# Layer B of a two-layer chunk-causal encoder: short value-product matmuls issued one by one between 512-column projection matmuls

## The chip, the cores and the metric

The kernel runs on one core of one Trainium2 chip, in one launch. The metric is the device time of that launch in microseconds; the number given is the median of several runs. One further execution was taken with the hardware profiler, and all rows of the profile come from that one.

## The reference, cut to what matters

Two layers are applied to 2048 prompt frames and 64 sample frames of width 1024. Each layer projects the normalised input to queries, keys, values and a gate, attends within a band of chunks of 64 frames, multiplies with the gate and projects back with a residual. Layer A has 16 query heads on 2 key heads and looks back 2 chunks; layer B, which the change names, has 16 heads of its own and looks back 8 chunks. For one chunk:

```python
s = jnp.einsum('bqkgd,bskd->bkgqs', qg, k).astype(jnp.float32) * (dh ** -0.5)
s = s + bias.reshape(kv, g, tq, tk)
p = jax.nn.softmax(s, axis=-1)
o = jnp.einsum('bkgqs,bskd->bqkgd', p.astype(v.dtype), v)   # the value product
y = x + (o * silu(gate)) @ w_out
```

Everything is float32. The kernel splits each factor into a high and a low part and adds up products of the parts, two or three matmuls for each product.

## The kernel before, in words

Tokens are handled in units of 256 (two tiles of 128), eight for the prompt, and a ninth unit of one tile with the 64 sample frames, which comes just ahead of the last prompt unit. Layer B runs eight passes, one for each pair of heads; in a pass it goes through the nine units. Each (pass, unit) is an item of the list `its`.

Two streams share TensorE, and the kernel writes TensorE's order out by hand (`tc.manual_schedule`); the orders on the other engines come from the scheduler. The first stream is the **filler** (`Filler`, L603): a list of jobs, each a generator that issues projection matmuls. `project` (L458) makes one tile's projection: eight blocks of the width, in each a high-by-high, a high-by-low and a low-by-high matmul of 512 columns (L473, L474, L475), 24 for a tile; for the sample tile the two parts of the input stand side by side in one operand and there are two matmuls for a block (L466 or L469, and L467). After each block the generator yields its cost, 3 x 512 / 2400 = 0.64 planner units, so `filler.step()` issues three matmuls at a time. `filler.done` counts the cost so far, `it.mark` is the count at which an item's projection is complete, and `filler.to(mark)` steps until the count is reached. When `filler.attending` is false, each step also drains some of the queued background work (`bg.drain`, L639).

The second stream is the attention of layer B (`pipeline`, L1189). An item has four heads in this sense (two tiles by two heads; the sample item two). For each of them the pipeline issues `scores` (L1070: matmuls L1100 and L1101, then a reduction on VectorE L1104 and an exponential on ScalarE L1108), then filler up to a first goal, then `values` for the head before (L1125: transposes L585 into the PSUM tile `sb`, split into high and low parts by ScalarE L557 and VectorE L558), then, after every second head, `outputs` (L1153), then filler up to a second goal. After head 1 of an item `queries` of the next one follows (L1032). A goal (L1209) is the smaller of two lines: from the count at the item's start, `c0`, to `end`, and, in the first four half-steps of an item, from `c0` to the mark of the item after next (`near`). `PACE_B` = 2.45 planner units for each head sets `end`, so an item of four heads asks for 9.8; `end` is at least the mark of the item after next.

`outputs` makes the value product of one head for a unit: for each tile of keys two matmuls, with the high part (L1178) and the low part (L1179) of the weights. Key tiles that both query tiles see take 256 columns. Up to two key tiles are seen by one query tile only: they take 128 columns and come last, two or four matmuls in a call. For the sample unit all six have 64 columns, and the last two of them have 64 rows, since the last block of keys is 64 long. For the second head of a pair `outputs` first transposes the gate (`tp`), and it ends with `finish_pairs` (L966): ScalarE copies (L971), VectorE additions (L973), a multiplication on GpSimd and a store.

In layer A the same filler runs under the attention of that layer (`pipeline`, L929), which places `values`, `keys`, `turned` and `outputs` at 0.3, 0.6, 0.8 and 0.95 of the way between two marks. After the attention of layer B the filler runs alone to its end with the output projection (L1301 to L1303, 264 columns).

Of the kernel before, what the change touches and what calls it, by code (L numbers as in the profile page):

```python
# [15 lines left out]
P = 128  # L16
D = 1024
KC = 8
# [30 lines left out]
NS = 4  # L49

@with_exitstack
def hybrid_encoder_kernel(
# [32 lines left out]
    nc = tc.nc  # L85
# [372 lines left out]
    def project(tile_, xc, w, C, res, ps=None):  # L458
        tt, t0, n = tile_
        ps = ps or psum("pj", 512, 2)  # L460
        for k in range(KC):
            wh, wl = weights_of(w, k)
            xh, xl = xc.parts[k // 2]
            if xl is None:
                if k == 0:
                    nc.tensor.matmul(ps[:, :C], xh[:, k % 2, :], wh, start=True, stop=False)  # L466
                nc.tensor.matmul(ps[:n, :C], xh[:, k % 2, :n], wl, start=False, stop=False)  # L467
                if k > 0:
                    nc.tensor.matmul(ps[:, :C], xh[:, k % 2, :], wh, start=False, stop=k == KC - 1)  # L469
                cost = 2 * C / 2400  # L470
            else:
                xh, xl = (a[:, k % 2, t0 : t0 + n] for a in (xh, xl))
                nc.tensor.matmul(ps[:n, :C], xh, wh, start=k == 0, stop=False)  # L473
                nc.tensor.matmul(ps[:n, :C], xh, wl, start=False, stop=False)  # L474
                nc.tensor.matmul(ps[:n, :C], xl, wh, start=False, stop=k == KC - 1)  # L475
                cost = 3 * C / 2400
            if k < KC - 1:
                yield cost
        res.append(ps)
        return cost  # L480

    def scaled(layer, tt, n, dst, ps):
        sc = rr[layer][:, tt : tt + 1]
# [162 lines left out]
    filler = Filler()  # L646
    finished = {}

    def layer_a():
# [4 lines left out]
        def add_unit(qd, place, unit):  # L654
            u, T, tiles = unit
            mine = []
            for tl in tiles:
                it = Item()
# [54 lines left out]
            def first():  # L713
                xc = st.x.pop((qd, u))
                pk = [psum("o", 512, 1), psum_a("sa", 512, 4)]
                kvs, qgs = [[], []], [[], []]
                yield from both([project(it.tile, xc, st.wkv, 256, o, ps) for it, o, ps in zip(mine, kvs, pk)])
                bias_vectors_a()
                keep(0)
                yield 2 * 3 * 256 / 2400  # L720
                for i, c in enumerate(both([project(it.tile, xc, st.w[qd], 512, o) for it, o in zip(mine, qgs)])):
                    if i == 7:
                        token_scales(unit, xc, psum("tp", 512, 1))
                        for it, o in zip(mine, kvs):
                            take_kv(it, o[0])
                    yield c
                for it, o in zip(mine, qgs):
                    take_qg(it, o[0])
                st.bias[0] = spread_first()
                token_scales(units[1], st.x[0, 1], psum("o", 512, 1))  # L730
                yield 2 * 3 * 512 / 2400

            def gen():
                xc = st.x.pop((qd, u))
# [243 lines left out]
    def layer_b():  # L978
# [171 lines left out]
                ))  # L1150
            it.sizes = sizes

        def outputs(it, h):  # L1153
            u, T, tiles = it.unit
            last = u == NU
            n = tiles[0][2]
            sizes = it.sizes
            if h == 0:
                it.O = psum("o", 512, 1)
            else:  # L1160
                GT = psum("tp", 512, 1)
                for e, (_, t0, _) in enumerate(tiles):
                    transpose(GT[:, t0 : t0 + n], it.G[:n, e * P : (e + 1) * P])
                gt = gate_t(GT[:, :T].rearrange("p (j s) -> p j s", j=1), T)
            mm = []
            if last:
                for c, kn in enumerate(sizes):
                    mm.append((VS[:kn, c, h], c, kn, 0, TS))
            else:
                ta, tb = tiles[0][0], tiles[1][0]  # L1170
                for kt in range(max(tb - 4, 0), ta + 1):
                    mm.append((VT[:, kt, h], kt - it.base, P, 0, UT))
                if ta >= 4:
                    mm.append((VT[:, ta - 4, h], ta - 4 - it.base, P, 0, P))
                mm.append((VT[:, tb, h], tb - it.base, P, P, UT))
            for x, (vt, c, kn, q0, q1_) in enumerate(mm):
                dst = it.O[:, h * T + q0 : h * T + q1_]
                nc.tensor.matmul(dst, vt, it.ph[h][:kn, c, q0:q1_], start=x == 0, stop=False)  # L1178
                nc.tensor.matmul(dst, vt, it.pl[h][:kn, c, q0:q1_], start=False, stop=x == len(mm) - 1)  # L1179
            if h == 1:  # L1180
                finish_pairs(
                    it.O[:, : 2 * T].rearrange("p (j e s) -> p j e s", j=1, e=2),
                    gt,
                    T,
                    og[1][:, it.hp : it.hp + 1, u * UT : u * UT + T],
                )
                finished[1, u] = finished.get((1, u), 0) + 1

        def pipeline():  # L1189
# [257 lines left out]
```

## Time and profile before

| | |
|---|---|
| median of 3 runs (lowest to highest) | 2319.13 us (2312.73 to 2319.27) |
| the profiled execution, its own time | 2308.83 us |
| its span from the first to the last instruction | 2307.1 us |
| busy: TensorE matmuls, its weight loads | 2266.7 us, 1986.4 us |
| busy: VectorE, ScalarE, GpSimd | 1562.2 us, 1439.4 us, 844.6 us |
| instructions | 42442, of them 13981 matmuls |

PE in the profile is TensorE's matmuls, PEld its weight loads, DVE is VectorE, ACT is ScalarE, POOL is GpSimd. A row of the timeline gives the start and the duration in microseconds, the engine, the line of the kernel, the operation, the output tile `<-` the inputs, and the shape; in a matmul's shape `128*128 128x256` the first pair is rows by columns of the stationary operand, and the last number is how many columns are streamed. Each matmul has a weight load of its own. Matmuls are pipelined, so durations of neighbours overlap: what one costs is read from the distance between starts, best over a stretch that begins and ends among long matmuls. A bracket gives the engine's idle time before the instruction and what ended it.

### The profile page before, as it was taken

To read this page: it belongs to the slowest core of one execution; us is meant where nothing else is said; L and a number is where in the kernel's file an instruction comes from. 1 tells how busy PE (TensorE), PEld (TensorE's weight loads), DVE (VectorE), ACT (ScalarE), POOL (GpSimd) and SP (SyncE) were. 2 spreads that over 40 slices of the span, in tenths; PEclk is the share of its full clock that TensorE was granted. 3 is DMA by queue.
4 is the path that set the end of the run, shared out by engine and by line. 5 is a ranking of instruction groups with operands and counts; after the bars stand their busy time and mean duration, and the time that the engine had idled before them with its cause. 6 is when DMAs were issued, how large, how long until landed. Compare 5 with 4: busy or idle time off the path is not lost.

```text
span 2307.1 us, 42442 instructions
## 1 busy us (share of the span) xinstructions
PE 2266.7 (98%) x13981; PEld 1986.4 (86%) x13981; DVE 1562.2 (68%) x5226; ACT 1439.4 (62%) x3640; POOL 844.6 (37%) x1186
## 2 busy tenths in 40 slices
PE   8999999999999999999999999999999999999999
PEld 6887788888889998888888888888888888888999
DVE  6778888888784447766766767767767677676211
ACT  6788777777774436765656656656656566565321
POOL 5554433333254446432222222222223222224443
PEclk9999999999999999999999999999999999999999
DMA  8746656544346767454443443444445335333664
GB/s 265 257 134 226 226 171 196 176 156 143 119 129 192 217 206 277 157 173 151 140 147 123 157 143 121 157 147 131 145 133 161 127 115 174 124 127 107 194 185 146
DMA packets 232126, 379.37 MB, mean 164 GB/s; under 512 B 24721, under 2 KB 163361, under 8 KB 231873
## 3 DMA queue, kind: packets, MB, share of 16 engines
q1 hardware_dynamic: 231904, 376.65, 51.7%
q8 instruction: 110, 1.80, 0.3%
q14 instruction: 112, 0.91, 0.1%
HBM read 296.13 MB, written 82.08 MB: 164 GB/s over the span
## 4 chain that ended last, share of the span: by engine, by line
PE 79%; DVE 7%; DMA 6%; ACT 5%; issue 2%; POOL 1%; SPq 0%; POOLq 0%; ACTq 0%; DVEq 0%
PE pj L473 13%; PE pj L475 12%; PE pj L474 12%; PE pj L1301 5%; PE sb L585 5%; PE pj L1302 5%; PE pj L1303 5%; PE o L1179 3%; PE o L1178 3%; PE sb L1100 3%; PE sb L1101 3%; PE tp L585 3%; PE sa L585 2%; DMA xraw<-in_x_rows_dram 1%; DMA row<-vec 1%
## 5 line engine op out<-in xcount | busy, mean ns | idle before, releaser
L473 PE MATMUL pj<-wh,xx 128*128 128x512 f32 (+1 forms) x1648 | 668.9, 406 | 9.9 <-DVE pb L488 3.9
L475 PE MATMUL pj<-wh,xx 128*128 128x512 f32 (+1 forms) x1648 | 639.2, 388 | 0.0
L474 PE MATMUL pj<-wl,xx 128*128 128x512 f32 (+1 forms) x1648 | 636.0, 386 | 1.4 <-DVE wl L306 1.4
L475 PEld LDWEIGHTS pj<-wh,xx 128*128 128x128 f32 x1648 | 310.8, 189 | 67.0
L473 PEld LDWEIGHTS pj<-wh,xx 128*128 128x128 f32 x1648 | 312.4, 190 | 51.0 <-ACT wh L303 4.1
L474 PEld LDWEIGHTS pj<-wl,xx 128*128 128x128 f32 x1648 | 312.9, 190 | 40.9 <-DVE wl L306 3.1
L377 POOL TENSOR_TENSOR xx<-xraw,xx 128x528 fp32r<-128x528 f32 (+1 forms) x200 | 265.7, 1345 | 203.6 <-ACT xx L376 191.2
L516 POOL TENSOR_TENSOR f<-f,mhalf 128x4 f32<-128x4 f32 (+3 forms) x221 | 228.5, 1034 | 220.3 <-DVE f L512 213.2
L1108 ACT ACTIVATE p<-p,nm 128x640 f32<-128x640 f32 (+5 forms) x272 | 204.4, 752 | 157.6 <-DVE nm L1104 155.5
L1301 PE MATMUL pj<-xx,wh 128*128 128x264 f32 x1024 | 294.1, 287 | 1.3 <-DVE res L1306 1.3
L1302 PE MATMUL pj<-xx,wh 128*128 128x264 f32 x1024 | 291.2, 284 | 0.0
L1303 PE MATMUL pj<-xx,wl 128*128 128x264 f32 x1024 | 289.9, 283 | 0.0
L558 DVE TENSOR_TENSOR pl<-sb,ph 128x640 fp32r<-128x640 f32 (+5 forms) x288 | 197.0, 684 | 126.2 <-ACT ph L557 123.8
L1104 DVE CUSTOM_DVE_ANT_0 p<-sb,BT 128x640 f32<-128x640 f32 (+5 forms) x272 | 196.8, 724 | 120.4 <-PE sb L1101 116.7
L557 ACT CAST ph<-sb 128x640 fp32r<-128x640 f32 (+5 forms) x288 | 167.3, 581 | 126.5 <-PE sb L585 118.5
L974 POOL TENSOR_TENSOR o<-gt,o 128x256 f32<-128x256 f32 (+2 forms) x140 | 107.1, 765 | 376.0 <-issue 158.3
L376 ACT CAST xx<-xraw 128x528 fp32r<-128x528 f32 (+1 forms) x200 | 122.3, 626 | 185.4 <-PE pj L1303 98.7
L1301 PEld LDWEIGHTS pj<-xx,wh 128*128 128x128 f32 x1024 | 192.8, 188 | 2.3 <-DVE res L1306 1.8
L1302 PEld LDWEIGHTS pj<-xx,wh 128*128 128x128 f32 x1024 | 192.5, 188 | 0.2
L1303 PEld LDWEIGHTS pj<-xx,wl 128*128 128x128 f32 x1024 | 192.6, 188 | 0.0
L1306 DVE TENSOR_TENSOR res<-pj,res 128x264 f32<-128x264 f32 x128 | 55.0, 430 | 200.7 <-PE pj L1303 197.6
L512 DVE CUSTOM_DVE_ANT_0 sq<-pa 128x64 f32<-128x64 f32 (+1 forms) x850 | 170.4, 253 | 23.3 <-ACT pa L485 21.3
(194 smaller groups left out, 4814.9 us busy)
## 6 DMA issues: line engine op xcount, KB each, us to landing
xx<-xsb SPq DMA_DIRECT2D x224, 512.0 KB, 4.0
xx<-xsa SPq DMA_DIRECT2D x88, 512.0 KB, 4.5
xraw<-oga SPq DMA_DIRECT2D x64, 264.0 KB, 3.4
xraw<-ogb SPq DMA_DIRECT2D x64, 264.0 KB, 3.2
xsa<-xx SPq DMA_DIRECT2D x32, 512.0 KB, 4.3
wraw<-in_w_in_b_dram SPq DMA_DIRECT2D x64, 256.0 KB, 3.5
xsb<-xx SPq DMA_DIRECT2D x32, 512.0 KB, 4.5
xraw<-in_x_dram SPq DMA_DIRECT2D x40, 256.0 KB, 3.9
```

The lines of the kernel that those rows point to most:

```text
L377: nc.gpsimd.tensor_tensor(xl, rv, xh.bitcast(F32), op=ALU.subtract)
L473: nc.tensor.matmul(ps[:n, :C], xh, wh, start=k == 0, stop=False)
L474: nc.tensor.matmul(ps[:n, :C], xh, wl, start=False, stop=False)
L475: nc.tensor.matmul(ps[:n, :C], xl, wh, start=False, stop=k == KC - 1)
L516: nc.gpsimd.tensor_tensor(fv, fv, mhalf[:n, :H], op=ALU.pow)
L558: b = nc.vector.tensor_tensor(dst_lo, src, dst_hi.bitcast(F32), op=ALU.subtract)
L585: nc.tensor.transpose(out, in_, ident[:n, :n])
L1104: mi = nc.vector.tensor_tensor_reduce(out=p[:n, :nk], in0=S[:n, o : o + nk], in1=bias[:n, b0 : b0 + nk], op0=ALU.add, op1=ALU.min, scale=1 ...
L1108: ex = nc.scalar.activation(p[:n, :nk], p[:n, :nk], AF.Exp, scale=-1.0, bias=nmh, accum_out=it.sm[:n, 2 * i + h : 2 * i + h + 1],)
L1301: nc.tensor.matmul(ps[:, :OT], wh, oh, start=k == 0, stop=False)
L1302: nc.tensor.matmul(ps[:, :OT], wh, ol, start=False, stop=False)
L1303: nc.tensor.matmul(ps[:, :OT], wl, oh, start=False, stop=k == KC - 1)
```

## The change

Each call of `filler.step()` issues one matmul of a projection where it issued a block of three (or two for the sample tile), and the generator yields after each with the cost of one, 512 / 2400 = 0.213. The order of the matmuls within a tile stays as it was. In `first`, where two tiles are projected in turn, the turns are now of one matmul, and the step at which the token scales follow is renumbered. `outputs` gets a function `between`, which it calls ahead of each matmul of at most 128 columns; the pipeline passes one that issues one filler matmul as long as the goal that comes next isn't reached. What is left to that goal follows after `outputs`, as before. The two high and low matmuls of `outputs` are written as one loop.

```diff
@@ project
+                xb = xh[:, k % 2, :]
+                mms = [(ps[:, :C], xb, wh), (ps[:n, :C], xb[:, :n], wl)]
+                if k:
+                    mms.reverse()
             else:
                 xh, xl = (a[:, k % 2, t0 : t0 + n] for a in (xh, xl))
-                nc.tensor.matmul(ps[:n, :C], xh, wh, start=k == 0, stop=False)
-                nc.tensor.matmul(ps[:n, :C], xh, wl, start=False, stop=False)
-                nc.tensor.matmul(ps[:n, :C], xl, wh, start=False, stop=k == KC - 1)
-                cost = 3 * C / 2400
-            if k < KC - 1:
-                yield cost
+                mms = [(ps[:n, :C], xh, wh), (ps[:n, :C], xh, wl), (ps[:n, :C], xl, wh)]
+            for y, (dst, a, b) in enumerate(mms):
+                end = k == KC - 1 and y == len(mms) - 1
+                nc.tensor.matmul(dst, a, b, start=k == y == 0, stop=end)
+                if not end:
+                    yield C / 2400
         res.append(ps)
-        return cost
+        return C / 2400
@@ first
-                yield 2 * 3 * 256 / 2400
+                yield 2 * 256 / 2400
-                    if i == 7:
+                    if i == 3 * 7:
-                yield 2 * 3 * 512 / 2400
+                yield 2 * 512 / 2400
@@ layer_b
-        def outputs(it, h):
+        def outputs(it, h, between=lambda: None):
...
-                nc.tensor.matmul(dst, vt, it.ph[h][:kn, c, q0:q1_], start=x == 0, stop=False)
-                nc.tensor.matmul(dst, vt, it.pl[h][:kn, c, q0:q1_], start=False, stop=x == len(mm) - 1)
+                for part in (it.ph[h], it.pl[h]):
+                    if q1_ - q0 <= P:
+                        between()
+                    nc.tensor.matmul(
+                        dst, vt, part[:kn, c, q0:q1_],
+                        start=x == 0 and part is it.ph[h], stop=x == len(mm) - 1 and part is it.pl[h],
+                    )
...
                 def goal(s):
-                    filler.to(c0 + min((end - c0) * s / (2 * len(heads)), (near - c0) * s / NS))
+                    return c0 + min((end - c0) * s / (2 * len(heads)), (near - c0) * s / NS)
...
-                    goal(2 * y + 1)
+                    filler.to(goal(2 * y + 1))
...
-                        outputs(*pend)
+                        outputs(*pend, lambda: filler.done < goal(2 * y + 2) - 0.01 and filler.step())
-                    goal(2 * y + 2)
+                    filler.to(goal(2 * y + 2))
```

More of the change, by code (lines that the diff above doesn't have):

```diff
@@ L464, in project @@
             if xl is None:
[L465 to L470, printed above, removed]
+                xb = xh[:, k % 2, :]
+                mms = [(ps[:, :C], xb, wh), (ps[:n, :C], xb[:, :n], wl)]
+                if k:
+                    mms.reverse()
             else:
                 xh, xl = (a[:, k % 2, t0 : t0 + n] for a in (xh, xl))
-                nc.tensor.matmul(ps[:n, :C], xh, wh, start=k == 0, stop=False)
-                nc.tensor.matmul(ps[:n, :C], xh, wl, start=False, stop=False)
-                nc.tensor.matmul(ps[:n, :C], xl, wh, start=False, stop=k == KC - 1)
-                cost = 3 * C / 2400
-            if k < KC - 1:
-                yield cost
+                mms = [(ps[:n, :C], xh, wh), (ps[:n, :C], xh, wl), (ps[:n, :C], xl, wh)]
[4 more added lines that the diff above has]
+                    yield C / 2400
         res.append(ps)
-        return cost
+        return C / 2400
     def scaled(layer, tt, n, dst, ps):
```

## The prediction

> **What bounds the kernel now.** I read the page first, then the busy time by stage, then the timeline around the value product.
>
> ```profile
> span 2307.1 us, 42442 instructions
> PE 2266.7 (98%) x13981; PEld 1986.4 (86%) x13981; DVE 1562.2 (68%) x5226; ACT 1439.4 (62%) x3640; POOL 844.6 (37%) x1186
> PEclk9999999999999999999999999999999999999999
> ```
>
> TensorE is busy for 98% of the span, and the granted clock is full in every slice. Of the profiled execution's 2308.83 us, 2307.1 are span and 1.7 lie around it; it stands 10.3 us, or 0.45%, below the median of the runs shown, 2319.13. The sum below is made against 2308.83 and then carried over to that median.
>
> ```profile
> core 0: us, PE busy (x) PEld busy (x) DVE busy (x) ACT busy (x) POOL busy (x), PEclk, DMA share, GB/s
> 890.00:2090.00 1200.00, 1191.18 (x6951) 1020.24 (x6951) 843.08 (x2846) 766.30 (x1927) 357.05 (x541) 1.00 0.45 145
> ```
>
> In layer B's attention TensorE idles for 8.8 us of 1200, while VectorE has work for 70% and ScalarE for 64%. So the change can win in two ways only: the same matmuls take less time on TensorE in another order, or idle time goes.
>
> **The change part by part.** *The short matmuls.* How many of 128 columns there are says the view of groups by shape, with as many for L1178:
>
> ```profile
> L1179 PE MATMUL o<-pl,VT 128*128 128x128 f32 x224 | 56.8, 275 | 0.0
> ```
>
> That makes 448 of 128 columns; by the code there are six of 64 columns in each of 16 sample calls, 96. The mean durations, 275 ns here, overlap and aren't what one costs. A call with four of them, in order of time:
>
> ```profile
> 1565.49 0.28 PE L1179 MATMUL o<-pl,VT 128*128 128x256 f32 x1
> 1565.61 0.22 PE L1178 MATMUL o<-ph,VT 128*128 128x128 f32 x1
> 1565.66 0.28 PE L1179 MATMUL o<-pl,VT 128*128 128x128 f32 x1
> 1565.78 0.28 PE L1178 MATMUL o<-ph,VT 128*128 128x128 f32 x1
> 1565.89 0.28 PE L1179 MATMUL o<-pl,VT 128*128 128x128 f32 x1
> 1566.00 0.45 PE L473 MATMUL pj<-wh,xx 128*128 128x512 f32 x1
> 1566.29 0.39 PE L474 MATMUL pj<-wl,xx 128*128 128x512 f32 x1
> 1566.52 0.39 PE L475 MATMUL pj<-wh,xx 128*128 128x512 f32 x1
> ```
>
> A matmul of 256 columns takes 0.12 us from start to start (1565.49 to 1565.61), one of 512 takes 0.23 (1566.29 to 1566.52). From 1565.49 to 1566.29 lie one of 256, the four short ones and one of 512: 0.80 - 0.12 - 0.23 = 0.45, or 0.112 us for each short one. By its columns it should take a quarter of 0.23, 0.058 us. What fills the rest? Weight loads, which start 0.11 us apart here:
>
> ```profile
> 1565.61 0.19 PEld L1179 LDWEIGHTS o<-pl,VT 128*128 128x128 f32 x1
> 1565.72 0.19 PEld L1178 LDWEIGHTS o<-ph,VT 128*128 128x128 f32 x1
> ```
>
> So a short matmul costs one weight load, 0.11 us, of which 0.054 isn't covered by its own columns. The question of the change is whether a long neighbour covers it. The load that is exposed is the one for the matmul *after* the short one: a long matmul ahead hides the short one's own load, but the next load then lies under 0.058 us of short matmul wherever it stands. If only one load goes ahead of a running matmul, the sum is the same for L S L S as for S S L L. The trace has the wanted pattern: single transposes of 128 columns between 512-column matmuls, 15 of them in layer A's first stage. The first and the last:
>
> ```profile
> 39.10 0.40 PE L475 MATMUL pj<-wh,xx 128*128 128x512 f32 x1
> 39.34 0.27 PE L585 MATMUL sa<-ident,pa 128*128 128x128 f32 x1
> 39.36 0.47 PE L473 MATMUL pj<-wh,xx 128*128 128x512 f32 x1
> 39.68 0.39 PE L474 MATMUL pj<-wl,xx 128*128 128x512 f32 x1
> ...
> 221.25 0.40 PE L475 MATMUL pj<-wh,xx 128*128 128x512 f32 x1
> ...
> 221.82 0.39 PE L474 MATMUL pj<-wl,xx 128*128 128x512 f32 x1
> ```
>
> 0.58 and 0.57 us for two long matmuls and the lone short one; less 2 x 0.23 that is 0.12 and 0.11. Standing alone saves nothing. In the changed program's order about 500 of the 544 have a projection matmul on both sides. Bounds: all of the uncovered 0.054 us saved, 448 x 0.054 = 24 us and for the 96 of 64 columns 96 x 0.08 = 8 us more, 32 us faster; and 0.01 us lost on each of 500, 5 us slower. I take the nearest row, 0.115 in the mean against 0.112: **+1.5 us**.
>
> *The 64-row matmuls.* A lone 64-row matmul between long ones, and the pair that ends a sample call:
>
> ```profile
> 201.22 0.40 PE L475 MATMUL pj<-wh,xx 128*128 128x512 f32 x1
> 201.55 0.28 PE L585 MATMUL sa<-ident,pa 64*128 64x64 f32 x1
> 201.76 0.50 PE L473 MATMUL pj<-wh,xx 128*128 128x512 f32 x1
> 202.09 0.39 PE L474 MATMUL pj<-wl,xx 128*128 128x512 f32 x1
> ```
> ```profile
> 1031.93 0.28 PE L1179 MATMUL o<-pl,VS 128*128 128x64 f32 x1
> 1032.14 0.29 PE L1178 MATMUL o<-ph,VS 64*128 64x64 f32 x1
> 1032.27 0.27 PE L1179 MATMUL o<-pl,VS 64*128 64x64 f32 x1
> 1032.47 0.50 PE L473 MATMUL pj<-wh,xx 128*128 128x512 f32 x1
> 1032.81 0.39 PE L474 MATMUL pj<-wl,xx 128*128 128x512 f32 x1
> ```
>
> The lone one costs 0.87 - 0.46 = 0.41 us. The pair: 0.88 us from the last 128-row short matmul to the second long one, where the run above took 0.40 (1565.89 to 1566.29), so 0.48 for two. Changing between 128 and 64 rows costs, and a pair pays once. The changed order puts a projection matmul between the two in 7 of the 16 sample calls: 7 x (2 x 0.41 - 0.48) = **+2.4 us**, between 0 and 16 x 0.34 = 5.4. The Trainium skill ("TensorE: Matmul & The Clock Gate", section "What happens when you issue a matmul") says that a weight load is pulled ahead of running matmuls when the row groups don't conflict. By that the switch need not cost and this term might be nothing; the rows speak against it.
>
> *The pace in layer B.* Steps of one matmul round less. An item of four heads asks for 9.8 units, 45.9 matmuls: in threes 48, in ones 46. A projected unit has 48 matmuls and the sample unit 16 where its item asks for 27; before, the filler therefore runs ahead by some 12 matmuls a pass until the second line of the goal (`near`) holds it back. In the order of before, heads 16 to 19 and 23 of passes 2 to 7 (counted from 0) then hold only 9, 9, 10, 8 and 9 projection matmuls; in pass 1 they hold 12, 12, 12, 10 and 12. In the changed order every such head holds 11 or 12. What thin heads cost shows when pass 1 stands beside passes 2 and 6, and head 17 of pass 1 beside that of pass 3:
>
> ```profile
> 1048.87:1205.53 156.66, 156.66 (x918) 134.95 (x917) 108.82 (x369) 97.84 (x247) 40.87 (x64) 1.00 0.44 141
> 1205.53:1361.21 155.68, 154.85 (x907) 132.62 (x906) 108.69 (x369) 97.86 (x247) 42.46 (x67) 1.00 0.44 140
> 1828.46:1984.11 155.65, 154.86 (x906) 132.63 (x905) 108.80 (x369) 97.80 (x247) 43.15 (x69) 1.00 0.44 139
> ```
> ```profile
> 1122.32:1128.19 5.87, 5.87 (x40) 5.26 (x39) 5.57 (x18) 5.02 (x13) 2.29 (x3) 1.00 0.44 132
> 1434.04:1440.49 6.45, 5.66 (x38) 4.69 (x36) 4.21 (x9) 4.04 (x9) 1.81 (x2) 1.00 0.73 231
> ```
>
> Pass 1 has 12 matmuls of 0.23 us more and should take 2.8 us more than the others; it takes 1.0 more. Pass 2 so loses 1.6 us, with 11 matmuls less, and pass 6 1.8, most of it in head 17, which needs 0.58 us more with three long matmuls (0.69) less: 1.3 us. In passes 2 to 6 that is 5 x 1.7 = 8.5; pass 7, where the output projection begins, I leave out. If the changed passes run as pass 1 does, **-8.5 us**; between -12 (the idle time of layer B with what follows each wait) and 0, if the wait moves to another head. For that the same work on ScalarE and VectorE must fit under heads of 11, which pass 1's 10 suggests.
>
> *Late outputs.* Up to four projection matmuls now stand ahead of the end of `outputs`, so its last matmul comes up to 0.9 us later, and with it ScalarE's copies L971, VectorE's L973 and the store on SyncE's queue, whose reader is the output projection much later. Queued behind them are the copies of `queries` and the next exponential. I cost this at nothing, covered by the six projection matmuls (1.4 us) between `scores` and `values`; the third rival is what it costs without that cover.
>
> *Layer A, start and end.* A tile's projection still is 24 matmuls between marks; `values` comes one matmul sooner, `turned` two, `outputs` one, so its distance of 15 from `values` stays. Loads and weight splits move with their steps by at most two long matmuls. While attention is off, each step runs at least one queued item, so items come up to three times as densely; it concerns the first some 40 us and the passage to layer B. I take 0, between -4 and +4.
>
> Sum: 1.5 + 2.4 - 8.5 = -4.6 us, 2304 for the profiled execution, **2314.5 us** from the median.
>
> **The rivals.** *The loads are hidden.* If a load could go two matmuls ahead, lone short ones would cost their columns: 32 us as bounded above, less 2.4, plus 8.5, some 38 us faster, 2281. For it speaks that all neighbours are long now; against it the lone transposes. The same section of the Trainium skill lets a load into the background weight buffer go ahead of running matmuls and doesn't say how many; by one, which the lone transposes bear out, this rival falls.
>
> *The waits move.* If the waits come from eight weight splits bunching on ScalarE and VectorE and not from thin heads, they come back in another head: 1.5 + 2.4 = +4, 2323.
>
> *The late outputs decide.* This one ends slower. Now, at a gated head:
>
> ```profile
> 1592.54 0.74 PE L585 MATMUL sb<-ident,p 128*128 128x128 f32 x5 [0.57 <-DVE nm L1104]
> 1596.18 0.85 DVE L973 TENSOR_TENSOR o<-o,o 64x256 f32<-64x256 f32 x2 [1.31 <-ACT o L971]
> 1597.18 0.83 DVE L1104 CUSTOM_DVE_ANT_0 p<-sb,BT 128x640 f32<-128x640 f32 x1 [0.15 <-PE sb L1101]
> ```
>
> L973 ends at 1597.03, 0.15 us before the next scores are there for L1104. With outputs 0.9 us later, L1104 starts 0.75 us late. The transposes waited for an L1104 once already in this item (1592.54): where they take the PSUM buffer that L1104 frees, they come 1.4 us after the scores and L1104 needs 0.83, so from 0.57 us of delay on TensorE waits. 0.2 us at each of 64 gated heads is 13 us; with +4 for the other terms and no gain, 2336.
>
> **How the numbers follow.** 0.3% is 7 us, about what a measurement of this kernel can tell from no change. The forecast has 0.55 (0.25 of it beyond 7 us faster, since -4.6 with bounds of 4 either way reaches there, 0.30 within); the moved waits 0.25 (0.24 within, 0.01 slower); the hidden loads 0.05; the late outputs 0.08; something in the start or layer A beyond its bounds 0.07 (0.04 faster, 0.03 slower). Faster 0.34, same 0.54, slower 0.12. The range 2302 to 2326 takes in the forecast with its bounds and the moved waits.
>
> **What would show it.** In the changed profile, a call's four short matmuls with four long ones should take 4 x (0.23 + 0.115) = 1.38 us; 1.16 would be hidden loads. TensorE's idle time in layer B should fall below half of 8.8 us, with no wait of the `sb` transposes on L1104's successor in head 17. The sample calls should show 0.41 us at each lone 64-row matmul. I am wrong if a lone short matmul costs clearly less than 0.11, or if the `sb` transposes wait at the gated heads.

## The result and the profile after

The changed kernel takes 2332.14 us (median; 2330.67 to 2333.95), the kernel before 2315.98 in the same comparison (2312.73 to 2319.27): ratio 1.0068, 95% interval 1.0056 to 1.0081, so 13 to 19 us slower, 16.2 by the medians. The forecast, 2314.5 with a range up to 2326, missed it on the side that had 0.12. The profiled execution took 2333.47 us, with a span of 2331.7.

Lines have moved: the transposes L585 are L583 after (L586 in most experiments), the splits L557/L558 are L555/L556 (L558/L559), the scores' reduction L1104 is L1102 (L1105), the exponential L1108 is L1106 (L1109), ScalarE's output copies L971 are L969 (L972), the low parts of `queries` L1061 are L1059 (L1062), the value product L1178/L1179 is L1179 (L1182 or L1186), and every projection matmul is L474.

From the page after, TensorE first:

```profile
span 2331.7 us, 42398 instructions
PE 2271.3 (97%) x13981; PEld 1985.6 (85%) x13981; DVE 1569.8 (67%) x5226; ACT 1439.8 (62%) x3640; POOL 837.5 (36%) x1186
```

The same 13981 matmuls stand in a span that is 24.6 us longer, and TensorE's busy time has grown by 4.6 of these: most of what was added is waiting. Layer B's attention after, pass 2 first and then 1200 us from its first scores on:

```profile
1219.18:1376.47 157.29, 155.38 (x906) 132.51 (x905) 109.29 (x371) 98.60 (x247) 41.50 (x67) 1.00 0.45 139
...
903.00:2103.00 1200.00, 1183.44 (x6889) 1009.52 (x6890) 835.34 (x2812) 760.70 (x1904) 343.20 (x532) 1.00 0.46 144
```

TensorE idles 16.6 us of 1200 where it idled 8.8; I had said below half of 8.8. Pass 2 takes 157.3 us instead of 155.7. Which waits these are, by engine and line (us in total, times, longest), over 1050 to 2000 us, first before, then after:

```profile
PE sb L585 <- DVE nm L1104: 2.8, 5, 0.6
PE o L1179 <- DVE pl L558: 1.2, 5, 0.2
```
```profile
PE sb L583 <- DVE pl L556: 8.0, 17, 1.2
PE tp L583 <- DVE KB L1059: 4.2, 6, 0.7
```

The wait at head 17 for the reduction is gone, as forecast. In its place the `sb` transposes wait for the low part of the head before (heads 3, 19 and 23 of a pass), and the gate's transposes for the low parts of `queries` (head 29).

**A trap in the pair of profiles.** Layer B's first scores come at 890.72 us before and at 903.15 after. That looks as if 12.4 of the 24.6 us were lost ahead of layer B. One of the experiments below (`e2_a_in_threes`) has the kernel before's order on TensorE, VectorE, ScalarE and GpSimd up to that point, row for row in the two traces. First scores before, then in that kernel:

```profile
890.72 0.30 PE L1100 MATMUL sb<-KA,q 128*128 128x128 f32 x1 [0.70 <-ACT pa L485]
```
```profile
900.28 0.28 PE L1101 MATMUL sb<-KA,q 128*128 128x128 f32 x1
```

The same work came 9.6 us later. One place of it is ScalarE waiting for a load of the input, before and in that kernel:

```profile
278.13 0.62 ACT L376 CAST xx<-xraw 128x512 fp32r<-128x512 f32 x1 [5.16 <-DMA xraw<-in_x_dram]
```
```profile
288.53 0.62 ACT L376 CAST xx<-xraw 128x512 fp32r<-128x512 f32 x1 [7.93 <-DMA xraw<-in_x_dram]
```

So the profiled execution of before was a lucky one: 2308.83 against a median of 2316, and the luck lies ahead of layer B. From the first scores to the end of the span, by contrast, kernels with the same layer B agree within 1 us. The table uses that column for layer B and the timed ratio for the whole.

| kernel (layer A; layer B) | median us | ratio, 95% interval | first scores us | from there to the end us |
|---|---|---|---|---|
| before (threes; threes) | 2315.98 | 1 | 890.7 | 1416.4 |
| changed (ones; ones, interleaved) | 2332.14 | 1.0068, 1.0056 to 1.0081 | 903.2 | 1428.5 |
| e1 (ones; ones) | 2319.81 | 1.0021, 1.0012 to 1.0030 | 899.6 | 1417.7 |
| e2 (threes; ones, interleaved) | 2328.52 | 1.0058, 1.0044 to 1.0071 | 900.3 | 1427.5 |
| e3 (ones; threes) | 2322.07 | 1.0021, 1.0006 to 1.0036 | 903.7 | 1416.6 |
| e4 (changed, sample unit in runs) | 2326.19 | 1.0051, 1.0038 to 1.0063 | 901.3 | 1424.2 |
| e9 (changed, 64-row pairs in runs) | 2323.09 | 1.0036, 1.0022 to 1.0050 | 897.3 | 1423.5 |
| e8 (threes; ones) | 2317.64 | 1.0008, 0.9997 to 1.0019 | 901.1 | 1417.1 |
| e6 (threes; ones, late but in runs) | 2323.54 | 1.0030, 1.0019 to 1.0041 | 897.0 | 1423.8 |
| e7 (threes; ones, value product ahead) | 2394.01 | 1.0333, 1.0320 to 1.0346 | 892.7 | 1500.3 |
| e5 (threes; threes, interleaved) | 2332.93 | 1.0065, 1.0051 to 1.0080 | 899.5 | 1431.5 |
| e11 (ones, drained by threes; threes) | 2318.20 | 1.0010, 1.0001 to 1.0019 | 899.9 | 1416.4 |
| e10 (e8, sample unit's filler later) | 2312.73 | 0.9988, 0.9977 to 1.0000 | 905.3 | 1414.1 |
| e12 (e10, two waits addressed) | 2307.22 | 0.9949, 0.9935 to 0.9964 | 898.3 | 1407.2 |

Ratios are to the kernel before, timed alongside on the same chip (its medians were 2315.5 to 2317.5); 0.001 is 2.3 us. "Ones" and "threes" are the matmuls in a filler step.

### The profile page after: what moved, and what is told of

Its sections match the earlier page's. It is cut to its first block, busy times and chain, and to the rows that moved or that the text cites. A ratio compares the mean times of both kernels' runs of the same rounds, so it can differ in the third digit from the quotient of the medians.

```text
span 2331.7 us, 42398 instructions
## 1 busy us (share of the span) xinstructions
PE 2271.3 (97%) x13981; PEld 1985.6 (85%) x13981; DVE 1569.8 (67%) x5226; ACT 1439.8 (62%) x3640; POOL 837.5 (36%) x1186
## 5 line engine op out<-in xcount | busy, mean ns | idle before, releaser
L474 PE MATMUL pj<-wh,xx 128*128 128x512 f32 (+1 forms) x3400 | 1143.8, 398 | 9.8 <-ACT wh L303 4.7
L474 PEld LDWEIGHTS pj<-wh,xx 128*128 128x128 f32 x3400 | 621.5, 189 | 116.0 <-ACT wh L303 6.6
L474 PE MATMUL pj<-wl,xx 128*128 128x512 f32 (+2 forms) x1752 | 691.2, 397 | 0.1
L474 PEld LDWEIGHTS pj<-wl,xx 128*128 128x128 f32 (+1 forms) x1752 | 325.5, 186 | 53.8 <-DVE wl L306 2.0
L1106 ACT ACTIVATE p<-p,nm 128x640 f32<-128x640 f32 (+5 forms) x272 | 204.5, 752 | 202.0 <-DVE nm L1102 198.0
L556 DVE TENSOR_TENSOR pl<-sb,ph 128x640 fp32r<-128x640 f32 (+5 forms) x288 | 197.4, 685 | 145.4 <-ACT ph L555 142.5
L1102 DVE CUSTOM_DVE_ANT_0 p<-sb,BT 128x640 f32<-128x640 f32 (+5 forms) x272 | 196.8, 724 | 73.0 <-PE sb L1099 67.9
L972 POOL TENSOR_TENSOR o<-gt,o 128x256 f32<-128x256 f32 (+2 forms) x140 | 102.2, 730 | 393.5 <-ACT pb L483 159.2
L555 ACT CAST ph<-sb 128x640 fp32r<-128x640 f32 (+5 forms) x288 | 167.3, 581 | 82.7 <-PE sb L583 74.7
L510 DVE CUSTOM_DVE_ANT_0 sq<-pa 128x64 f32<-128x64 f32 (+1 forms) x850 | 175.6, 258 | 28.1 <-ACT pa L483 27.7
L583 PEld LDWEIGHTS sb<-ident,p 128*128 128x128 f32 (+2 forms) x1168 | 138.9, 140 | 59.3 <-DVE pl L556 23.9
L583 PE MATMUL sb<-ident,p 128*128 128x128 f32 (+2 forms) x1168 | 171.8, 272 | 12.2 <-DVE pl L556 10.9
```

The lines of the kernel that those rows point to most:

```text
L474: nc.tensor.matmul(dst, a, b, start=k == y == 0, stop=end)
L510: nc.vector.tensor_tensor_reduce(out=sq[:n, c], in0=src[:, c], in1=src[:, c], op0=ALU.mult, op1=ALU.add, scale=1.0, scalar=HD * EPS, accum ...
L555: a = nc.scalar.copy(dst_hi, src)
L556: b = nc.vector.tensor_tensor(dst_lo, src, dst_hi.bitcast(F32), op=ALU.subtract)
L583: nc.tensor.transpose(out, in_, ident[:n, :n])
L1102: mi = nc.vector.tensor_tensor_reduce(out=p[:n, :nk], in0=S[:n, o : o + nk], in1=bias[:n, b0 : b0 + nk], op0=ALU.add, op1=ALU.min, scale=1 ...
```

## The experiments

### Interleaving or step size, layer A or layer B

The first theory, from the two profiles, was that most of the loss came from the finer steps in layer A. The rivals were the interleaving and the finer pace of layer B. `e1_runs_of_short` takes the interleaving out of the changed kernel:

```diff
-                        between()
+                        pass
```

> The steps stay one matmul long in both layers; the short matmuls of the value product go back into runs. Three theories of where the +16 us of the change come from. Layer A (the finer steps move the work of layer A against its waits: layer B's first scores came at 903.2 us in the profile after, 890.7 before, 12.4 us later): this kernel keeps the loss, first scores near 903, time 2328 to 2334. Interleaving (late outputs, which delay ScalarE's copies, exponentials and splits): the loss goes with it, time 2316 to 2320, and the waits of the transposes at heads 19 and 23 in layer B, 0.75 us each in a pass after, are gone. Finer pace of layer B (fewer matmuls ahead of a head's transposes): waits at heads 3, 19, 23 and 29 stay, 3 us in a pass.

2319.81 us, ratio 1.0021, and 1417.7 us from the first scores on, against 1428.5. The interleaving costs 10.8 us there; the layer A theory, which wanted 2328 or more, falls as the main cause. It gets one thing right: 1.0021 isn't 1. Of the waits, the interleaving theory wanted those at heads 19 and 23 gone. Over 1050 to 2000 us the `sb` transposes' waits for low parts fall from 8.0 us to 3.1: those at head 3 go, at head 19 two short ones are left, but head 23 still waits 0.4 us in each pass, and the 4.2 us of head 29 stay. These belong to the pace.

`e2_a_in_threes` gives `project` a flag and yields once for three matmuls in layer A, so that only layer B is changed:

```diff
-                if not end:
-                    yield C / 2400
+                if single:
+                    if not end:
+                        yield C / 2400
+                elif y == len(mms) - 1 and not end:
+                    yield len(mms) * C / 2400
```

> Layer A's projection steps are three matmuls long again, as before; layer B keeps steps of one matmul and the interleaving. Layer A theory: first scores of layer B back near 891 us, time 12 us below the changed kernel's 2332.1, so near 2320. Interleaving or pace of layer B: the time stays above 2328, and the first scores matter little.

2328.52 us, ratio 1.0058. Above 2328, as the rivals wanted, and the first scores at 900.3 showed the trap told above.

`e3_a_single_only` is the mirror: ones in layer A, threes and no interleaving in layer B.

> Only layer A has steps of one matmul; layer B has steps of three and no interleaving, as before. Layer A theory: first scores of layer B near 903 us, time 12 us above the 2316.0 of the kernel before, so near 2328, and passes of layer B of 155.7 us as before. Interleaving or pace of layer B: time 2314 to 2319.

2322.07 us, between the two expectations; 1416.6 us in layer B, as before (1416.4). So layer A's part is real (the interval begins at 1.0006) but under half of the 12 us that the pair of profiles suggested.

### Late outputs, lone short matmuls, or the pace

`e8_single_b_no_mix` is e2 without the interleaving, so that only the pace of layer B is finer.

> Layer A with steps of three, layer B with steps of one and the short matmuls in runs: the finer pace of layer B alone. The prediction gave this -8.5 us (0 to -12), since the heads with 8 or 9 projection matmuls become heads with 11 or 12. The runs so far (steps of one in both layers without interleaving 1.0021, in layer A alone 1.0021) say that it is worth 0: 2314 to 2318, because the wait of 1.2 us at head 17 goes and waits of 0.6 and 0.8 us at heads 23 and 29 come. If the prediction's term is right after all: 2306 to 2309.

2317.64 us, ratio 1.0008, 1417.1 us in layer B: the finer pace is worth nothing (+0.7 us), where the prediction had -8.5. The waits over 1050 to 2000 us:

```profile
PE tp L586 <- DVE KB L1062: 4.2, 6, 0.7
PE sb L586 <- DVE pl L559: 2.8, 8, 0.4
```

`e6_late_run` separates lateness from standing alone: ahead of the first short matmul of a call it issues, in one row, as many projection matmuls as the interleaving would, and then the short ones in a run.

```diff
                     if q1_ - q0 <= P:
-                        between()
+                        if not run:
+                            run = 2 * sum(m[4] - m[3] <= P for m in mm)
+                            for _ in range(run):
+                                between()
```

> Layer A with steps of three as before, layer B with steps of one. The projection matmuls that stood between the short ones now stand ahead of the first short one in one row, and the short ones in a row behind them: the value product ends as late as with the interleaving, but no short matmul stands alone. To be read beside the same kernel with the interleaving (2328.5 us, 1.0058 of before) and without it. Late-outputs theory (the value product ends 1 to 3 us later, and with it the copies, additions and splits on ScalarE and VectorE for which the next transposes wait): the loss stays but for the parted 64-row matmuls, 2324 to 2328, with waits of the transposes at heads 3, 19 and 23 of a pass as with the interleaving. Rival, that lone short matmuls themselves are dear: 2314 to 2319, as without the interleaving.

2323.54 us, ratio 1.0030, half a microsecond below the range of the late-outputs theory and well above its rival's. In layer B 1423.8 us, 6.7 more than e8: issuing the value product late, with no short matmul alone, makes over half of the loss there. 4.9 of the 6.7 us are idle time of TensorE (20.9 against 16.0 us from the first scores on). The waits of the transposes for the low part go from 2.8 us to 7.3, the other stays at 4.2:

```profile
PE sb L586 <- DVE pl L559: 7.3, 19, 1.0
```

How a late value product makes the transposes wait is seen at heads 18 and 19 of pass 4. In e8 head 18's scores start at 1604.27 and ScalarE works through a queue without a gap:

```profile
1603.01 0.75 ACT L972 COPY o<-o 64x256 f32<-64x256 f32 x2
1603.78 0.72 ACT L303 ACTIVATE wh<-wraw,gain 128x512 fp32r<-128x512 f32 x1
1604.53 0.58 ACT L486 ACTIVATE pa<-pj,rms 128x384 f32<-128x384 f32 x1
...
1607.15 0.83 ACT L1109 ACTIVATE p<-p,nm 128x640 f32<-128x640 f32 x1
...
1608.09 0.69 ACT L558 CAST ph<-sb 128x640 fp32r<-128x640 f32 x1
```
```profile
1608.82 0.82 DVE L559 TENSOR_TENSOR pl<-sb,ph 128x640 fp32r<-128x640 f32 x1 [0.17 <-ACT ph L558]
```
```profile
1610.27 0.71 PE L586 MATMUL sb<-ident,p 128*128 128x128 f32 x5
```

The low part is done at 1609.64, 0.63 us ahead of the next transposes. In e6 head 18's scores start at 1603.26, 1.01 us earlier on that execution's clock, while the later work on ScalarE happens to stand at the same times, so it comes later after the scores:

```profile
1603.02 0.73 ACT L303 ACTIVATE wh<-wraw,gain 128x512 fp32r<-128x512 f32 x1 [0.73 <-DMA wraw<-in_w_in_b_dram]
1603.77 0.75 ACT L972 COPY o<-o 64x256 f32<-64x256 f32 x2
1604.55 0.58 ACT L486 ACTIVATE pa<-pj,rms 128x384 f32<-128x384 f32 x1
...
1607.16 0.83 ACT L1109 ACTIVATE p<-p,nm 128x640 f32<-128x640 f32 x1
...
1608.11 0.70 ACT L558 CAST ph<-sb 128x640 fp32r<-128x640 f32 x1
```
```profile
1608.83 0.82 DVE L559 TENSOR_TENSOR pl<-sb,ph 128x640 fp32r<-128x640 f32 x1
```
```profile
1609.71 0.77 PE L586 MATMUL sb<-ident,p 128*128 128x128 f32 x5 [0.32 <-DVE pl L559]
```

Counted from head 18's scores, the copies L972 begin at +0.51 instead of -1.26 and the projection's evacuation L486, the exponential and the high and low parts come 1.0 us later. The 0.63 us that the transposes had are used up and TensorE waits.

The copies come 1.77 us later here, though the value product itself ends only 0.9 us later (its last matmul starts 1.90 us ahead of the scores in e8 and 0.99 in e6). The rest is the order of ScalarE's queue, which the scheduler made anew: the cast of weights L303 that stands behind the copies in e8 stands ahead of them in e6 and first waits 0.73 us for its load (the bracket above). The changed kernel has the same order there, with 0.4 to 1.1 us of such waits in passes 2 to 5. Of the 4.9 us of added idle time some 3.3 stand at head 19, behind this place.

At head 3, where e6 waits 0.2 us in a pass and e8 not at all, the delay runs along VectorE's queue. For head 2 of pass 4 the additions L974 begin 0.61 us after its scores instead of 0.32 ahead of them, and the reduction, the parts of `queries` and the low part follow almost without a gap, the low part 0.7 us later than in e8. There too something came ahead: L522, which waits for GpSimd and stands behind the additions in e8. What the late value product would cost with e8's orders on ScalarE and VectorE no run shows.

`e7_outputs_first` puts the interleaved value product ahead of a head's first goal and ahead of `values`:

```diff
+                    if pend is not None:
+                        filler.to(goal(2 * y + 1) - (12 if pend[0].unit[0] == NU else 4) * 512 / 2400)
+                        outputs(*pend, lambda: filler.done < goal(2 * y + 1) - 0.01 and filler.step())
                     filler.to(goal(2 * y + 1))
```

> Layer A in threes, layer B in ones, short and 512-column matmuls interleaved, but the whole value product stands ahead of the first goal of a head and ahead of the next transposes, so that it ends earlier than before the change by some 1 us and its copies come before the next splits. Late-outputs theory: the loss of the interleaving but for the 64-row matmuls (3 to 4 us) goes, 2317 to 2321, and the waits at heads 3 and 19 are gone. Rival, lone short matmuls dear: 2326 to 2330, as with the interleaving behind. A third outcome, the transposes coming later and the value product of the next head meeting its splits: waits of the value product on VectorE's low parts, over 2330.

2394.01 us, the third outcome and far beyond it: from 1050 to 2000 us the value product itself waits for the low parts that it reads, since only a half-step is left for the splits:

```profile
PE o L1182 <- DVE pl L559: 33.2, 29, 2.1
```

From the first scores on it takes 71.8 us more than the changed kernel, of which 48 are idle time of TensorE; the rest isn't explained. Earlier in this place is no cure; of the two theories this kernel tells nothing.

`e5_between_threes` leaves all steps at three and interleaves blocks.

> All steps of three as before, with blocks of three between the short matmuls while the goal allows it: the pace of before, the value product as late as with the interleaving, but only two blocks for four short matmuls. Late-outputs theory: 2322 to 2328. Rival, lone short matmuls dear: half of them stand alone, 2319 to 2322. If the finer pace is what makes the late outputs harmful (11 instead of 12 matmuls in every second head): 2315 to 2319.

2332.93 us, above what the late-outputs theory wanted, and 1431.5 us in layer B, 3 more than the changed kernel. With fewer lone short matmuls than the changed kernel, 180 against 519 by the traces, it loses more, so lone short matmuls aren't the cause, and the finer pace isn't what makes late outputs harmful. Here the transposes wait for the reduction, in the place that the prediction's third rival named:

```profile
PE sb L586 <- DVE nm L1105: 5.1, 10, 0.7
PE sb L586 <- ACT sq L530: 3.5, 5, 0.7
```

### The 64-row matmuls

`e4_sample_in_runs` keeps the sample unit out of the interleaving (`if q1_ - q0 == P`), and `e9_rows64_in_runs` only its two 64-row matmuls (`and kn == P`).

> The changed kernel, but the value product of the sample unit (64 columns, the last two matmuls with 64 rows) stays in runs, so that no two 64-row matmuls are parted. By the prediction's term this takes back 7 of 16 partings at 0.34 us, 2.4 us: 2329.7. If a parting costs nothing, or the loss lies elsewhere, 2332; if lone 64-row matmuls are the whole loss, 2316.

> The changed kernel with one exception: ahead of the two 64-row matmuls of the sample unit no projection matmul is put, so that no two of them are parted; the other ten short matmuls of that unit stay between projection matmuls. With the sample unit's whole value product in runs the ratio was 1.0051 instead of 1.0068, 4 us. If the parted 64-row matmuls are that 4 us: 1.0051 again, 2327 to 2329, and from layer B's first scores to the last matmul 1420 us, as there, instead of 1424.6. If it is the sample unit's late value product instead: 1.0066 to 1.0070, 2331 to 2333, and 1424.

e4 took 2326.19 us, e9 2323.09; in layer B 1424.2 and 1423.5 us against 1428.5. Keeping the pair together gives back all that the sample unit loses, 4.3 to 5.0 us; e4 and e9 both came 3.5 to 4 us below their expected times (2329.7 and 2327), and why isn't known. The layer B column is free of what happens ahead of layer B. e9 also equals e6 (1423.8), which parts no pair and has every short matmul in a run: with the 64-row pairs out of it, interleaving costs what lateness costs. Of the 5.0 us by e9, 3.0 are busy time of TensorE (1406.1 against 1403.1 us from the first scores on) and 2.0 are idle time (22.4 against 20.4).

### Layer A

`e11_drain_by_threes` is e3 with the background work drained once in three steps:

```diff
-            if not self.attending:
-                bg.drain(FR * c)
+            self.owed += c
+            self.steps += 1
+            if self.steps % 3 == 0:
+                if not self.attending:
+                    bg.drain(FR * self.owed)
+                self.owed = 0.0
```

> Layer A in steps of one, layer B as before, but the background work is drained once for three steps with the budget of three, where each drain rounds up to a whole job. The same kernel with a drain for each step took 1.0021 of before, 4.9 us more, and its TensorE waited 11.0 us in layer A for the head norm's outputs (transposes into tp), which kernels with steps of three do for 0 to 1.4 us. If the drains make the loss: 2315 to 2318 and under 2 us of those waits. If it is the places of the transposes and the other work of layer A, which come up to two matmuls sooner as a goal is no longer overshot: 2319 to 2323, and 7 to 11 us of those waits.

2318.20 us, at the edge of the first expectation and below the second, ratio 1.0010 (1.0001 to 1.0019) against 1.0021 (1.0006 to 1.0036): the times don't tell the two apart. The waits do. TensorE's up to 890 us, in e3 and then in e11:

```profile
PE tp L586 <- DVE pa L522: 11.0, 5, 3.5
```
```profile
PE tp L586 <- DVE pa L522: 7.9, 4, 3.3
```

A second wait of these transposes, for `sm`, is 7.0 us in both. Most of the waits stay without the dense drains, so the drains make at most a small part of them. The kernels with threes wait at other places instead, for instance e2 in the value product, 6.0 us for high and 4.5 us for low parts.

### A version below both

What is left in each pass of e8 is a wait at head 29 (0.69 us idle, the gate's transposes) and one at head 23 (0.36 us idle, the `sb` transposes). `e10_sample_later` lowers the goal of the sample unit's first head, so that more filler stands ahead of the gate's transposes:

```diff
+                if len(heads) == 2:
+                    near -= 1.5
```

> A try at a version below both: layer A in threes, layer B in ones without interleaving (1.0008 of before), and at the sample unit's first head the goal is lowered, so that 7 instead of 10 projection matmuls stand there and 21 instead of 18 at its second head, 14 instead of 11 of them ahead of the gate's transposes, which wait 0.77 us for the queries' low parts in each of eight passes. If that wait goes and nothing takes its place: 6 us less, 2309 to 2313, 0.998. If the transposes of the first head, now with 4 matmuls ahead of them, wait instead: 2316 to 2319.

2312.73 us, ratio 0.9988 with an interval that just reaches 1; layer B 1414.1 us. The wait falls from 4.2 us to 1.5 in the stretch used above, and doesn't go: the three matmuls only changed heads, so the gate's transposes stand as far behind head 28's scores as in e8, and what helps is that `queries`, and with it the last low part, comes 0.42 us sooner. `e12_two_waits` goes on from there:

```diff
-                    near -= 1.5
+                    near -= 2.2
...
-                    filler.to(goal(2 * y + 1))
+                    filler.to(goal(2 * y + 1) + (0.43 if y == 3 else 0))
```

> The version of 0.9988 of before (layer A in threes, layer B in ones without interleaving, 7 and 21 projection matmuls at the sample unit's two heads) with its last two steady waits of a pass addressed: 0.35 us of the gate's transposes at head 29 by 5 and 23 matmuls, 16 instead of 14 of them ahead of the transposes; and 0.62 us of the transposes at head 23, which wait for the low part of the head before, by 8 instead of 6 matmuls ahead of a unit's fourth transposes and 3 or 4 instead of 5 or 6 behind its value product, whose result nothing waits for until the other head of the pair. If both waits go: 1 us in each of seven to eight passes, 2306 to 2310, 0.995 to 0.997, and passes of 154.2 us instead of 155.1. If the second only moves to the next head: 2310 to 2313.

2307.22 us, ratio 0.9949 (0.9935 to 0.9964): 8 to 15 us below the kernel before and some 25 below the changed one, which was timed in another comparison. Over 1050 to 2000 us one wait is left:

```profile
PE sb L586 <- DVE pl L559: 0.3, 1, 0.3
```

Layer B takes 1407.2 us, 9.2 less than before. Against e10, heads 28 and 29 together go from 10.5 to 10.2 us in a pass and head 23 from 5.7 to 5.2, so both edits give a part of it.

## Why the prediction was wrong

From -4.6 us forecast to 16.2 measured are 20.8 us. Two steps failed: the pace, forecast at -8.5 us, gave +0.7, and the late outputs, costed at nothing, gave +6.7. A third term, the 64-row matmuls, was too small by 2.6 us, and layer A wasn't nothing.

- **Lone short matmuls, +1.5 us: right in that standing alone saves nothing.** Four short and four long ones take 1.38 us after, from 1482.97 to 1484.35, the forecast figure. The whole term is -0.3 us by e9 less e6, nothing within the 1 us by which kernels with the same layer B differ:

```profile
1482.97 0.22 PE L1179 MATMUL o<-ph,VT 128*128 128x128 f32 x1
1483.03 0.45 PE L474 MATMUL pj<-wh,xx 128*128 128x512 f32 x1
1483.32 0.22 PE L1179 MATMUL o<-pl,VT 128*128 128x128 f32 x1
...
1484.07 0.45 PE L474 MATMUL pj<-wh,xx 128*128 128x512 f32 x1
1484.35 0.33 PE L1098 MATMUL sb<-KA,q 128*128 128x384 f32 x1
```

- **64-row matmuls, +2.4 us: right in kind, too small.** It is 4.3 to 5.0 us by e4 and e9, within the bound of 5.4. A parted pair after:

```profile
1044.99 0.47 PE L474 MATMUL pj<-wh,xx 128*128 128x512 f32 x1
1045.39 0.29 PE L1179 MATMUL o<-ph,VS 64*128 64x64 f32 x1
1045.61 0.49 PE L474 MATMUL pj<-wl,xx 128*128 128x512 f32 x1
1046.04 0.29 PE L1179 MATMUL o<-pl,VS 64*128 64x64 f32 x1
1046.26 0.45 PE L1098 MATMUL sb<-KA,q 128*128 128x384 f32 x1
1046.55 0.34 PE L1099 MATMUL sb<-KA,q 128*128 128x384 f32 x1
```

  From 1044.99 to 1046.55 are 1.56 us; less two long ones (0.46) and one of 384 columns (0.17), that leaves 0.93, or 0.46 for each 64-row matmul instead of 0.41. Seven partings at 2 x 0.46 - 0.48 are 3.1 us, and the busy time of e9 and the changed kernel differs by 3.0. The other 2.0 us are idle time at the waits of heads 3 and 19, which two kernels with the same layer B (the changed one and e2, 22.4 and 21.6 us idle) have unequal by 0.9 as well. So the term as the prediction meant it measured 3.0; why the waits are longer stays open.
- **Pace, -8.5 us: failed; it was +0.7 (e8), which is not clear of nothing.** The step "if the changed passes run as pass 1 does" failed. Thin heads did cause the wait at head 17, and it went. But the lead that made them thin also left 27 projection matmuls for head 29, and these covered the low parts of `queries`. With 18 there the gate's transposes wait 0.7 us in every pass, and at head 23 the `sb` transposes wait for a low part. In e8 TensorE's idle time is 2.5 us longer than before (16.0 against 13.5 us from the first scores on) and its busy time 1.8 us shorter. This is the second rival, "the waits move", as e8 shows alone. Pass 1, which the prediction took as its model, has 27 matmuls at head 29 too; pass 0, which has 21 there, showed the wait already before:

```profile
1025.42 0.41 PE L585 MATMUL tp<-ident,G 128*128 128x128 f32 x2 [0.47 <-DVE KB L1061]
```

- **Late outputs, 0: failed; it was +6.7 (e6 less e8).** The step was "covered by the six projection matmuls (1.4 us) between `scores` and `values`". That is the wrong cover: what counts is the time left between the end of a low part and the next transposes. It can be read where no view lists a wait yet. Before, at heads 18 and 19 of pass 4:

```profile
1600.69 0.82 DVE L558 TENSOR_TENSOR pl<-sb,ph 128x640 fp32r<-128x640 f32 x1
```
```profile
1601.57 0.77 PE L585 MATMUL sb<-ident,p 128*128 128x128 f32 x5
```

  The low part ended at 1601.51 and the transposes came 0.06 us later. That is no slack at all: transposes that the views list as waiting for a low part start as far behind its end (1609.65 to 1609.71 in e6). The idle time here was too short for the list, and a microsecond of delay had no room. The third rival (0.08) was the right kind: its additions hold up the reduction ahead of head 3. Its end was another: in the changed kernel the transposes wait for the low part, which comes later in the same queue, and not for L1104's successor, and at three heads of a pass instead of eight. What nothing in the prediction had is the work that comes ahead of the late copies and additions in their queues, above all the cast of weights at head 18. How the 6.7 us divide between the delay itself and these orders stays open.
- **Layer A, 0 (-4 to +4): about +2 to +5.** Pairs that differ only there differ in their ratios by 0.0021 (e3 to before), 0.0013 (e1 to e8) and 0.0010 (the changed kernel to e2). Only the first is clear of nothing by itself; the intervals of the other two pairs overlap. Steps of one move the waits to the transposes into `tp`. That the cause is their place, up to two matmuls sooner, is argued from e11 (the drains make little of these waits); it was not tried by itself.

Together: -0.3 + 5.0 + 0.7 + 6.7 = 12.1 us in layer B, and 2 to 5 ahead of it, 14 to 17 for 16.2. That the first sum is what was measured is no test: each term is the difference of two kernels of one chain from before to the changed kernel, so they are bound to add up. One thing more misled the reading of the result, though no term of the forecast: the profiled execution of before was 7 us under its median by luck ahead of layer B, which showed only when the same order had been profiled again.

## What to carry to other kernels

Before an instruction is delayed, follow everything behind it on the *other* engines' queues to the next point where the critical engine reads it, and subtract ends from starts there: no slack and 2 us of slack look alike in a table of waits. Then look for what may slip in ahead of the delayed work on its own queue. A wait that went because its head got more cover took that cover from another head here, so look at which head gives it. And profile one order of work twice before explaining a difference of a few microseconds between two profiles.

## What the runs showed of the hardware

Two things were not expected. A 512-column matmul ahead of a lone 64-row one takes 0.40 us to the next start (1044.99 to 1045.39 above) and the one between two of them 0.43, where 0.23 is usual. The Trainium skill ("TensorE: Matmul & The Clock Gate", section "What happens when you issue a matmul") has weight loads pulled ahead where row groups don't conflict or where they go to the background weight buffer. The first case is not met here, since the 64 rows lie among the 128 of the neighbours, so the prediction's "need not cost" did not follow from that one. By the rows above, a change from 128 rows to 64 isn't covered by a long matmul. The rows are what counts and not the 64 columns: in the same call a lone 64-column matmul of 128 rows and the long one behind it take 0.34 us together (1043.93 to 1044.27), where a 64-row one and the long one behind it take 0.65 (1045.39 to 1046.04).

The second is what follows a long wait. After 6.25 us of idle time in layer A of the changed kernel, the granted clock (the column behind the five engines) is 0.50 for 4 us. It was 1.00 after a wait of 3.41 us earlier in the same layer:

```profile
292.18 0.66 PE L583 MATMUL tp<-ident,pa 128*128 128x128 f32 x2 [6.25 <-DVE sm L885]
```
```profile
189.00:191.00 2.00, 1.97 (x11) 1.67 (x12) 0.31 (x5) 1.98 (x8) 1.00 (x1) 1.00 0.62 183
292.00:296.00 4.00, 3.82 (x11) 3.23 (x12) 1.67 (x6) 1.32 (x3) 0.61 (x1) 0.50 0.94 341
```

In these 4 us, 512-column matmuls start 0.43 us apart (294.35 to 294.78) instead of 0.23. If all of these 4 us did the work of 2, the wait cost about a third more than its idle time, by estimate. The page's row of the clock, in slices of 58 us, shows a 9 there, which can't tell a full clock from one that falls for a few microseconds. The kernel before has such stretches too, though the prediction read its row as full in every slice: 0.50 from 281.0 to 284.4 us, behind a wait of only 2.29 us. The waits in layer B, at most 1.4 us, have no such trail. The same page of the Trainium skill (section "What's actually happening") says that the array falls to half its clock after an idle window of about 3.4 us and comes back after as long a busy one. For the wait of 6.25 us the trace agrees (0.50 from 289.5 us, 3.6 us after the last matmul, until 296.3, 4.1 us after the next). The other two show that the length of a wait alone doesn't decide it here.
